# Two stacked transformer blocks on one core: the order of loads and small steps in the first layer's opening

## The chip, the core and the metric

The program runs on one core of a Trainium2 chip. Five engines work side by side, each through its own list of instructions in order: TensorE (PE; its weight loads are shown as PEld), VectorE (DVE), ScalarE (ACT), GpSimd (POOL) and SyncE (SP), which here only issues DMA transfers. ACT and POOL can issue transfers too. The metric is device time in microseconds (us) of one execution.

## What is computed

The reference is a first block of two layers followed by a second block of one layer, all on 256 tokens of width 1024 in float32. Only the opening of the first layer is touched:

```python
# layer 0 of the first block (S = 256 tokens, D = 1024)
h = rmsnorm(x, a_norm_attn);  z = h @ a_w_in           # q, k, v of 6 double heads, and qm
q, k = rope(q), rope(k)
o_self = diff_attention(q, k, v, lam, subln)           # 6 heads
kv = rmsnorm(mem, a_mem_norm) @ a_w_mem_kv             # 256 memory tokens
o_mem = softmax(qm @ mk.T / 8) @ mv                    # 4 memory heads
x = x + concat(o_self, o_mem) @ a_w_out                # then an MLP, layer 1, the second block
```

## The kernel before

**Products.** Every float32 weight tile arrives by DMA as `raw` (128 x 1024 floats, 512 KB, four buffers) and is split into a rounded part `hi` (one ACT instruction, L206) and a remainder `lo` (two DVE instructions, L216). The activations are split in the same way (`hA`, `hMa`, `hMb`: index 0 is the high part, 1 the remainder), and a product is three matmuls: hi by high, hi by remainder, lo by high. One weight tile is one *unit* of 24 matmuls of 256 columns. `tok_block` (L446) yields tokens x features, `feat_block` (L428) features x tokens; each takes two units, and keeps two PSUM tiles until its result is copied out (`evac`).

**Order.** The program has no scheduler at run time: the order in which this Python code emits instructions is the order on each engine. `run_plan` (L228) walks the units. `Order` (L43) holds a clock `O.t` that each matmul advances by its columns / 2.4 ns (four times as much for plain float32, L150), and a queue of generators with due times: `yield 600` means "go on when O.t is 600 ns later", a string means "when this is marked". After each group of matmuls `O.poll()` emits what is due, and at most one piece (hi or half of lo) of a coming weight tile is emitted; the lead over the unit being multiplied grows from 2.25 tiles to 4. `O.need(key)` (L97) emits whatever is queued until the key is marked. A `w_load` follows the last piece of each tile, on SP's queue, where it waits for its buffer.

**The opening before.** `first_inputs` (L895) issues the gains `par` on ACT's queue and, on SP's, x and the first block's weights in turns of two chunks (256 KB each). It emits ten warming matmuls, splits x and these weights two chunks at a time, and spawns:

- `squares`: the squares of x by ACT (L299), summed by POOL (L303, L305) into `ssq_A`; then `tok_stat` and `row_stat` with a delay of 3500, which put tiny products with ones (`mst`, `ms`) on PE and make from them tA (per token, needed to copy v out) and rA (per column, needed for qm, q and k, and by `tables`, four POOL instructions, `ropeR`).
- `second_inputs`: the memory tokens `memT` (1 MB) at once, the rope tables, lambda and constants later.
- `memory_a` at 9200: splits memT to `hMa` chunk by chunk (ACT, then DVE, L277), squares by ACT, sums by POOL (`ssq_M`); then row and token statistics M.
- `lambdas` at 15000; `memory_b` after the memory product.

The units of layer 0 are numbered here from 0: v blocks 0 to 5, qm 6 and 7, memory keys 8 and 9, memory values 10 and 11, then q and k of head h at 12 + 2h, the second layer's memory product, and the output product. A q and k block ends in `rope` (L586): two DVE and two POOL instructions for q, the same for k. `head_a` (the head's scores S, softmax and so on) is due 6500 after its block, `mem_pair` (the memory heads) after heads 0 and 1.

Of the kernel before, what the change touches and what calls it, by code (L numbers as in the profile page):

```python
# [108 lines left out]
def block_kernel(ctx: ExitStack, tc: tile.TileContext, a, out):  # L109
# [60 lines left out]
    def hook(fn):  # L170
        plan.append((len(wlist), 0, fn))

    def w_load(part=(), last=True):
        i = wstate.loaded
        if i >= len(wlist):
            return
        src = wlist[i]
        if i not in wstate.raws:
            wstate.raws[i] = wpool.tile(list(src.shape), F32, tag="raw", name="raw", bufs=RAW)
        sl = (slice(None),) + part  # L180
        nc.sync.dma_start(wstate.raws[i][sl], src[sl])
        wstate.loaded += last

    def w_split(i, part):
# [101 lines left out]


    class Stat:
        def __init__(self, name):
            self.acc = big.tile([P, S], F32, tag="ssq", name="ssq_" + name, bufs=2)  # L290
            self.first = None
            self.n = 0

        def add(self, src, keep=False):
            if keep:
                sq = w_tile("sqk", bufs=KC)
            else:
                sq = wk.tile([P, S], F32, tag="sq", name="sq", bufs=4)
            nc.scalar.activation(sq, src, AF.Square)  # L299
            if self.n == 0:  # L300
                self.first = sq
            elif self.n == 1:
                nc.gpsimd.tensor_tensor(self.acc, self.first, sq, OP.add)  # L303
            else:
                nc.gpsimd.tensor_tensor(self.acc, self.acc, sq, OP.add)  # L305
            self.n += 1
            return sq

# [134 lines left out]
                        O.give("acc", len(c0s))  # L443
            unit([src[:, k0:k0 + per, :]], fn)

    def tok_block(src, cols, h, evac, tile_fn=acc_tile, after=None):  # L446


        def late(dsts, what):
# [6 lines left out]
        for k0 in (0, 4):  # L456
            def fn(w, k0=k0):
                what = "ps" if tile_fn is ps_tile else "acc"
                if k0 == 0:
                    O.take_now(what, 2)  # L460
                    st.ps = [tile_fn("tp") for _ in range(2)]
                x = h()
                for k1 in (k0, k0 + 2):
                    half = w[k1 - k0:k1 - k0 + 2]
                    for j in range(2):
                        dst = st.ps[j][:, 0:cols]
                        ts = slice(j * P, (j + 1) * P)
                        for i, (hi, lo) in enumerate(half):
                            mm(dst, x[:, 0, k1 + i, ts], hi, start=(k1 + i == 0), stop=False)
                            mm(dst, x[:, 1, k1 + i, ts], hi, start=False, stop=False)  # L470
                        yield
                        for i, (hi, lo) in enumerate(half):
                            mm(dst, x[:, 0, k1 + i, ts], lo, start=False, stop=(k1 + i == KC - 1))
                        if j:
                            yield
                if k0 == 4:
                    dsts = [t[:, 0:cols] for t in st.ps]
                    if after:
                        O.spawn(late(dsts, what))
                    else:  # L480
                        for j in range(2):
                            evac(j, dsts[j])
                        O.give(what, 2)
# [410 lines left out]

    def first_inputs():  # L895
        nc.scalar.dma_start(par[:, 0:C_LAM], a["par"][:, 0:C_LAM])
        for i in range(4):
            nc.sync.dma_start(xT[:, 2 * i:2 * i + 2, :], a["xT"][:, 2 * i:2 * i + 2, :])
            w_load((slice(2 * (i % 2), 2 * (i % 2) + 2),), i % 2)
        w_load()  # L900
        w_load()
        E.hA = operand("hA")
        stA = Stat("A")
        warm = ps_tile("warm")
        for _ in range(10):
            nc.tensor.matmul(warm[:, 0:P], ones, ones, start=True, stop=True)
        for k in range(KC):
            split_scaled(E.hA, k, xT[:, k, :], gain(G_A_ATTN, k))
            if k % 2:
                w_split(k // 4, slice(k % 4 - 1, k % 4 + 1))  # L910
        w_piece()
        w_piece()
# [5 lines left out]
        def squares():  # L918
            for k in range(KC):
                stA.add(xT[:, k, :])  # L920
                yield 450
            O.spawn(tok_stat(stA, "A", 3500))
            O.spawn(row_stat(stA, "A", tables, 3500))

        def second_inputs():
            nc.sync.dma_start(memT, a["memT"])
            yield 8100
            nc.sync.dma_start(E.rope_a, a["rope_a"])
            nc.sync.dma_start(par[:, C_LAM:C_END], a["par"][:, C_LAM:C_END])
            nc.sync.dma_start(cst, a["cst"])  # L930

        O.spawn(squares())
        O.spawn(second_inputs())
        E.v = p_tile("vA", (P, 2, 768))
        E.o = operand("oA")
        O.spawn(lambdas(), 15000)
        O.spawn(bias_rows(), 40000)
        O.spawn(memory_a(), 9200)
        O.spawn(memory_b())

    def lambdas():
# [46 lines left out]
    hook(first_inputs)  # L988
    for i in range(3):
        tok_block(a["w_a_v"][i], 256, lambda: E.hA, scaled_tok(lambda: E.v, 256 * i, "tA"),  # L990
                  acc_tile if i else ps_tile, "tA")
    mem_queries(a["w_a_qm"], lambda: E.hA, "rA")
    mem_kv(a["w_a_mem"], wait_for("hMa", lambda: E.hMa), "ma")
    for h in range(6):
        qk_block(a["w_a_qk"][h], lambda: (E.hA, E.hA), wait_for("rA", lambda: E.tr),
                 lambda q, k, h=h: head_a(h, q, k), 6500)
        if h in (0, 1):
            hook(lambda h=h: O.spawn(mem_pair(h, "ma", 6 + h, "oA", PAUSE_MA)))
    mem_kv(a["w_b_mem"], wait_for("hMb", lambda: E.hMb), "mb")

    def staged(first, stat, g, last, name, also=None):
# [574 lines left out]
```

## Time and profile before

| | us |
|---|---|
| timed runs, median of 3 (lowest to highest) | 949.86 (949.54 to 951.19) |
| the profiled execution, its own time | 952.14 |
| its span, first to last instruction | 950.4 |
| TensorE busy in the span | 925.7 |
| first matmul of a product starts | 6.88 |
| output product of layer 0 starts | 128.60 |
| mean granted TensorE clock | 0.991 |

All rows are of the profiled execution; times in them count from its first instruction. An idle time in brackets is that of the engine before the instruction, with what ended it. A matmul of a profile row that names several is a merged run of them (x4), and its time runs from the first start to the last end.

### The profile page before, as it was taken

The numbers are of one execution on the slowest core, as the hardware profiler recorded it, in microseconds if no ns is written. First come the engines' busy times: TensorE is split into PE (matmuls) and PEld (weight loads), VectorE is DVE, ScalarE is ACT, GpSimd is POOL, SyncE is SP. The second block draws the span as 40 slices with busy tenths as digits, with TensorE's granted clock in tenths as the row PEclk, the third lists the DMA queues.
The fourth block names the chain that finished last, engine by engine and source line by source line (L and its number), as shares of the span: only waits on it lengthen the run. The fifth ranks groups of instructions, "written<-read, shape, count | busy, mean of one in ns | idle before, by whom it ended". The sixth has DMA issues, their size and how long they took to land.

```text
span 950.4 us, 17785 instructions
## 1 busy us (share of the span) xinstructions
PE 925.7 (97%) x6800; PEld 856.6 (90%) x6800; DVE 689.2 (73%) x1434; ACT 550.0 (58%) x1063; POOL 198.4 (21%) x236
## 2 busy tenths in 40 slices
PE   7899999999999999999999999999998999999998
PEld 7897898999999998888999999999887989999998
DVE  6978978766666697876866666688956788666664
ACT  6747666655555574656655555566476656555551
POOL 3414633000000032322000000055656411101010
PEclk9899999999999999999999999999999999999999
DMA  8553444665555535332675555574413456655551
GB/s 287 196 178 116 135 152 130 203 203 192 195 188 192 183 131 183 107 109 96 201 241 179 177 181 193 190 257 145 135 62 113 154 154 202 214 193 171 196 201 45
DMA packets 45686, 161.10 MB, mean 170 GB/s; under 512 B 5128, under 2 KB 6800, under 8 KB 45216
## 3 DMA queue, kind: packets, MB, share of 16 engines
q1 hardware_dynamic: 45104, 158.14, 50.6%
q0 software_dynamic: 208, 1.63, 0.6%
q8 instruction: 53, 0.87, 0.4%
q14 instruction: 33, 0.27, 0.1%
q10 hardware_dynamic: 288, 0.18, 0.1%
HBM read 158.88 MB, written 2.63 MB: 170 GB/s over the span
## 4 chain that ended last, share of the span: by engine, by line
PE 82%; DVE 8%; POOL 4%; ACT 2%; issue 2%; DMA 2%; DVEq 0%; SPq 0%; POOLq 0%; ACTq 0%
PE fp L149 41%; PE acc L149 31%; PE tp L149 3%; DVE lo L216 2%; PE S L149 2%; DMA raw<-in_w_a_v_dram 1%; POOL rsh L591 1%; DVE xT L569 1%; ACT hi L206 1%; PE O L149 1%; PE ms L149 1%; PE T L154 1%; PE Sm L149 1%; POOL ssq_A L305 1%; DVE hV L581 1%
## 5 line engine op out<-in xcount | busy, mean ns | idle before, releaser
L216 DVE TENSOR_TENSOR lo<-raw,hi 128x512 fp32r<-128x512 f32 (+1 forms) x555 | 381.8, 734 | 134.2 <-ACT hi L206 133.9
L206 ACT ACTIVATE hi<-raw 128x1024 fp32r<-128x1024 f32 x287 | 296.1, 1053 | 124.1 <-PE fp L149 51.2
L149 PE MATMUL acc<-u,hi 128*128 128x256 f32 x1376 | 245.0, 281 | 0.0
L149 PEld LDWEIGHTS acc<-u,hi 128*128 128x128 f32 x1376 | 210.7, 188 | 0.0
L149 PE MATMUL acc<-u,lo 128*128 128x256 f32 x688 | 193.3, 281 | 0.0
L149 PEld LDWEIGHTS acc<-u,lo 128*128 128x128 f32 x688 | 130.1, 189 | 0.0
L149 PE MATMUL fp<-hW,hi 128*128 128x512 f32 x352 | 96.5, 395 | 1.5 <-DVE uc L424 1.1
L421 ACT ACTIVATE uc<-fp 128x256 f32<-128x256 f32 x108 | 39.9, 380 | 68.9 <-PE fp L149 68.8
L149 PE MATMUL fp<-hV,hi 128*128 128x512 f32 x256 | 70.8, 396 | 0.5 <-DVE hV L581 0.4
L149 PE MATMUL fp<-hU,hi 128*128 128x512 f32 x256 | 70.7, 396 | 0.5 <-DVE hU L581 0.4
L149 PEld LDWEIGHTS fp<-hW,hi 128*128 128x128 f32 x352 | 60.1, 189 | 10.3 <-DVE hW L581 1.6
L424 DVE TENSOR_TENSOR uc<-fp,uc 128x256 f32<-128x256 f32 x108 | 44.2, 420 | 32.8 <-ACT uc L421 31.9
L149 PEld LDWEIGHTS fp<-hW,lo 128*128 128x128 f32 x352 | 53.9, 188 | 7.4
L149 PE MATMUL fp<-hW,lo 128*128 128x256 f32 x352 | 56.1, 282 | 0.0
L149 PEld LDWEIGHTS fp<-hV,hi 128*128 128x128 f32 x256 | 43.8, 189 | 6.9 <-DVE hV L581 1.6
L149 PEld LDWEIGHTS fp<-hU,hi 128*128 128x128 f32 x256 | 43.8, 189 | 6.9 <-DVE hU L581 1.6
L149 PE MATMUL fp<-hZ,hi 128*128 128x256 f32 x304 | 46.8, 294 | 0.4 <-DVE hZ L581 0.4
L857 POOL TENSOR_TENSOR uc<-uc,rstd_W 128x256 f32<-128x256 f32 x22 | 16.1, 754 | 147.8 <-ACT uc L855 147.8
L842 ACT ACTIVATE uu<-uc 128x256 f32<-128x256 f32 x64 | 24.1, 418 | 35.4 <-DVE uc L838 35.4
L149 PEld LDWEIGHTS fp<-hV,lo 128*128 128x128 f32 x256 | 39.2, 188 | 5.5
L149 PEld LDWEIGHTS fp<-hU,lo 128*128 128x128 f32 x256 | 39.2, 188 | 5.4
L564 DVE TENSOR_TENSOR u<-uu,u 128x256 fp32r<-128x256 f32 x64 | 24.4, 422 | 25.5 <-ACT u L562 25.5
(341 smaller groups left out, 1644.5 us busy)
## 6 DMA issues: line engine op xcount, KB each, us to landing
raw<-in_w_a_up_dram SPq DMA_DIRECT2D x32, 512.0 KB, 4.6
raw<-in_w_a_down_dram SPq DMA_DIRECT2D x32, 512.0 KB, 4.4
raw<-in_w_b_up_dram SPq DMA_DIRECT2D x32, 512.0 KB, 4.5
raw<-in_w_b_down_dram SPq DMA_DIRECT2D x32, 512.0 KB, 4.4
raw<-in_w_gate_dram SPq DMA_DIRECT2D x22, 512.0 KB, 4.5
raw<-in_w_up_dram SPq DMA_DIRECT2D x22, 512.0 KB, 4.7
raw<-in_w_down_dram SPq DMA_DIRECT2D x22, 512.0 KB, 4.0
raw<-in_w_a_qk_dram SPq DMA_DIRECT2D x12, 512.0 KB, 3.9
```

Source lines behind the costliest of these rows:

```text
L149: nc.tensor.matmul(dst, lhsT, rhs, **kw)
L154: nc.tensor.transpose(dst, src, ident)
L206: nc.scalar.activation(hi, raw, AF.Copy)
L216: eng.tensor_tensor(lo[sl], raw[sl], f32v(hi[sl]), OP.subtract)
L305: nc.gpsimd.tensor_tensor(self.acc, self.acc, sq, OP.add)
L421: nc.scalar.activation(c, p[:, S:2 * S], AF.Copy)
L424: nc.vector.tensor_tensor(c, p[:, 0:S], c, OP.add)
L564: nc.vector.tensor_tensor(u[:, 1, n, :], us[n], f32v(u[:, 0, n, :]), OP.subtract)
L569: nc.vector.tensor_tensor(x, bank, x, OP.add)
L581: nc.vector.scalar_tensor_tensor(h[:, 1, k, :], xT[:, k, :], g(k), f32v(h[:, 0, k, :]), OP.mult, OP.subtract)
L842: nc.scalar.activation(u, t, AF.Square)
L857: nc.gpsimd.tensor_tensor(g, g, rs, OP.mult)
```

## The change

The opening of the first layer is rearranged; arithmetic and results are the same.

1. The first transfers are smaller and come from two queues: chunk 0 of x and of the weights (128 KB each) on SP, chunk 1 of both on ACT behind `par`; the rest on SP as before.
2. The first v block is split and multiplied chunk by chunk: `w_split` takes chunks 0 and 1 singly, and `fine` makes `tok_block` emit all six matmuls of a chunk before the next.
3. The sums of squares of x go to DVE (`Stat("A", nc.vector)`).
4. `memT` comes in two halves, each 4000 later, behind the tables. `memory_a` is due at 22000 instead of 9200, `lambdas` at 17000 instead of 15000, the statistics A 7600 after the squares instead of 3500.
5. The memory product (keys and values) follows the second q and k block: units 6 and 7 are qm, 8 to 11 the q and k blocks of heads 0 and 1, 12 to 15 memory keys and values. The memory heads start after it and after head 2's block.

```diff
-    def w_load(part=(), last=True):
+    def w_load(part=(), last=True, queue=None):
...
-        nc.sync.dma_start(wstate.raws[i][sl], src[sl])
+        (queue or nc.sync).dma_start(wstate.raws[i][sl], src[sl])
...
-        def __init__(self, name):
+        def __init__(self, name, engine=None):
+            self.engine = engine or nc.gpsimd
...
-                nc.gpsimd.tensor_tensor(self.acc, self.acc, sq, OP.add)
+                self.engine.tensor_tensor(self.acc, self.acc, sq, OP.add)
...
-    def tok_block(src, cols, h, evac, tile_fn=acc_tile, after=None):
+    def tok_block(src, cols, h, evac, tile_fn=acc_tile, after=None, fine=False):
...
-                for k1 in (k0, k0 + 2):
+                for k1 in range(k0, k0 + 4) if fine else ():
+                    hi, lo = w[k1 - k0]
+                    for j in range(2):
+                        dst = st.ps[j][:, 0:cols]
+                        ts = slice(j * P, (j + 1) * P)
+                        mm(dst, x[:, 0, k1, ts], hi, start=(k1 == 0), stop=False)
+                        mm(dst, x[:, 1, k1, ts], hi, start=False, stop=False)
+                        mm(dst, x[:, 0, k1, ts], lo, start=False, stop=(k1 == KC - 1))
+                    yield
+                for k1 in () if fine else (k0, k0 + 2):
...
-        for i in range(4):
+        nc.sync.dma_start(xT[:, 0, :], a["xT"][:, 0, :])
+        w_load((slice(0, 1),), False)
+        nc.scalar.dma_start(xT[:, 1, :], a["xT"][:, 1, :])
+        w_load((slice(1, 2),), False, nc.scalar)
+        for i in range(1, 4):
...
-        stA = Stat("A")
+        stA = Stat("A", nc.vector)
...
-            if k % 2:
+            if k < 2:
+                w_split(0, slice(k, k + 1))
+            elif k % 2:
...
-            O.spawn(tok_stat(stA, "A", 3500))
-            O.spawn(row_stat(stA, "A", tables, 3500))
+            O.spawn(tok_stat(stA, "A", 7600))
+            O.spawn(row_stat(stA, "A", tables, 7600))
...
-            nc.sync.dma_start(memT, a["memT"])
             yield 8100
...
+            for i in range(2):
+                yield 4000
+                nc.sync.dma_start(memT[:, 4 * i:4 * i + 4, :], a["memT"][:, 4 * i:4 * i + 4, :])
...
-        O.spawn(lambdas(), 15000)
+        O.spawn(lambdas(), 17000)
...
-        O.spawn(memory_a(), 9200)
+        O.spawn(memory_a(), 22000)
...
-                  acc_tile if i else ps_tile, "tA")
+                  acc_tile if i else ps_tile, "tA", i == 0)
...
-    mem_kv(a["w_a_mem"], wait_for("hMa", lambda: E.hMa), "ma")
...
-        if h in (0, 1):
-            hook(lambda h=h: O.spawn(mem_pair(h, "ma", 6 + h, "oA", PAUSE_MA)))
+        if h == 1:
+            mem_kv(a["w_a_mem"], wait_for("hMa", lambda: E.hMa), "ma")
+        if h in (1, 2):
+            hook(lambda h=h: O.spawn(mem_pair(h - 1, "ma", 5 + h, "oA", PAUSE_MA)))
```

## Rows read from the trace of the kernel before

**Rows 1.** The page's busy times: us, share of the span, instructions.
```profile
PE 925.7 (97%) x6800; PEld 856.6 (90%) x6800; DVE 689.2 (73%) x1434; ACT 550.0 (58%) x1063; POOL 198.4 (21%) x236
```

**Rows 2.** Stretches: busy of PE, PEld, DVE, ACT, POOL; clock; DMA share; GB/s.
```profile
4.02:7.43 3.41, 1.49 (x12) 1.28 (x11) 1.45 (x3) 2.00 (x5) 0.00 (x0) 1.00 0.90 292
...
7.43:10.85 3.42, 3.42 (x17) 3.24 (x16) 3.00 (x7) 2.98 (x8) 0.00 (x0) 0.50 1.05 373
...
14.41:22.03 7.62, 4.89 (x42) 4.69 (x41) 6.74 (x7) 5.58 (x10) 7.10 (x7) 1.00 0.91 314
...
35.14:41.57 6.43, 4.21 (x34) 3.80 (x32) 6.40 (x13) 4.46 (x8) 5.45 (x8) 1.00 0.37 113
...
41.57:48.40 6.83, 6.42 (x28) 6.24 (x29) 6.66 (x18) 3.25 (x6) 0.00 (x0) 0.50 0.61 191
...
53.46:128.60 75.14, 72.01 (x577) 63.69 (x575) 65.48 (x155) 48.46 (x130) 35.16 (x43) 1.00 0.43 135
...
128.60:950.40 821.80, 808.53 (x5909) 748.96 (x5907) 582.08 (x1202) 467.14 (x868) 144.49 (x168) 1.00 0.51 168
```

**Rows 3.** Waits of TensorE, first 130 us: total us, times, longest.
```profile
PE mst L149 <- POOL ssq_A L305: 2.7, 1, 2.7
...
PE fp L149 <- DVE hMa L277: 2.6, 2, 2.2
```

**Rows 4.** Timeline of TensorE: start, us, instructions (xcount) [idle before].
```profile
14.41 0.64 PE L149 MATMUL tp<-hi,hA 128*128 128x256 f32 x4
...
22.03 0.61 PE L149 MATMUL mst<-ones,ssq_A 128*128 128x2 f32 x4 [2.73 <-POOL ssq_A L305]
...
22.50 0.68 PE L149 MATMUL ms<-ssq_A,ones 128*128 128x256 f32 x2
...
29.65 1.11 PE L149 MATMUL fp<-hA,hi 128*128 128x256 f32 x8
...
35.25 1.11 PE L149 MATMUL fp<-hMa,hi 128*128 128x256 f32 x8
...
43.21 1.05 PE L149 MATMUL ms<-ssq_M,ones 128*128 128x256 f32 x2
...
67.46 0.49 PE L149 MATMUL S<-k,q 64*128 64x128 f32 x4
...
68.84 0.72 PE L149 MATMUL fp<-hA,hi 128*128 128x256 f32 x4
```

**Rows 5.** Timeline of ScalarE, the opening.
```profile
11.19 0.62 ACT L191 ACTIVATE hi<-raw 128x512 fp32r<-128x512 f32 x1
...
24.74 1.57 ACT L800 ACTIVATE vA<-tp,rstdt_A 128x256 f32<-128x256 f32 x4
```

**Rows 6.** Timeline of VectorE, 11 to 36 us.
```profile
11.84 0.69 DVE L192 TENSOR_TENSOR lo<-raw,hi 128x512 fp32r<-128x512 f32 x1
...
23.55 0.68 DVE L216 TENSOR_TENSOR lo<-raw,hi 128x512 fp32r<-128x512 f32 x1
...
24.15 0.16 DVE L329 TENSOR_TENSOR rs4t<-rs4y 128x4 f32<-128x4 f32 x1
...
25.64 0.42 DVE L329 TENSOR_TENSOR rs256t<-rs256y 128x256 f32<-128x256 f32 x1
...
30.34 2.26 DVE L216 TENSOR_TENSOR lo<-raw,hi 128x512 fp32r<-128x512 f32 x2 [0.27 <-ACT hi L206]
...
32.53 0.77 DVE L942 CAST identb<-cst 128x128 bf16<-128x128 f32 x1
...
35.43 0.47 DVE L277 SCALAR_TENSOR_TENSOR hMa<-memT,par,hMa 128x256 fp32r<-128x256 f32 x1
```

**Rows 7.** Timeline of GpSimd, 33 to 63 us.
```profile
33.87 3.78 POOL L305 TENSOR_TENSOR ssq_M<-ssq_M,sq 128x256 f32<-128x256 f32 x4
...
59.32 0.73 POOL L591 TENSOR_TENSOR rsh<-rsh,ropeR 128x256 f32<-128x256 f32 x1 [18.34 <-DVE rsh L590]
...
61.82 1.05 POOL L592 TENSOR_TENSOR k<-rt,rsh 128x256 f32<-128x256 f32 x1
```

More of the change, by code (lines that the diff above doesn't have):

```diff
@@ L302, in add @@
             elif self.n == 1:
-                nc.gpsimd.tensor_tensor(self.acc, self.first, sq, OP.add)
+                self.engine.tensor_tensor(self.acc, self.first, sq, OP.add)
             else:
-                nc.gpsimd.tensor_tensor(self.acc, self.acc, sq, OP.add)
+                self.engine.tensor_tensor(self.acc, self.acc, sq, OP.add)
             self.n += 1
```

## The prediction

> **What bounds the kernel now.** I read the page's busy times first, then a table of stretches, then the waits of TensorE, and last the timelines of the stretches where TensorE waits. TensorE is busy for 925.7 of 950.4 us [rows 1], and of the 821.8 us behind the output product of layer 0 only 13.3 are idle [rows 2]: nothing of the change lies there. What it can win lies ahead of 128.6. Up to 4.02 only warming runs. In 4.02 to 7.43 TensorE is busy 1.49 us and waits 1.92 for the first chunks; the clock then falls to 1.2 GHz (0.50) for 3.41 us, although TensorE is busy throughout [rows 2]. From 14.41 to 22.03 it is busy 4.89 of 7.62 us: it waits 2.7 for GpSimd's sum of squares [rows 2, 3]. From 35.14 to 41.57 it is busy 4.21 of 6.43 and waits for VectorE's remainders of the memory tokens, 2.6 in all, and the clock is at 0.50 for the next 6.83 us [rows 2, 3]. From 53.46 to 128.6 the idle rest is 3.1 us in 75.1 [rows 2]. So the opening loses 2.7 + 2.6 in waits and half of (3.4 + 6.8) to the clock, besides the time until the first product (6.88 in the table). The reader is to see next to it that VectorE was busy for 6.40 of the 6.43 us in which TensorE waited for it [rows 2]: it was not slow with one thing, it was behind with everything.
>
> **1. Opening.** The smaller first transfers and the split by chunks let the first product start earlier, at about 5.5 instead of 6.88. But the first block ends no sooner than its last data. These come in the same bytes at the same rate: the DMA engines are at 0.90 and 1.05 of their time from 4.02 to 10.85 [rows 2], so I count no gain for them. ACT then splits the last two weight chunks from 11.19 to 11.81 and VectorE their remainders to 12.53 [rows 5, 6]. Two of the twelve matmuls of these chunks can run ahead of that; the other ten take 1.2 us (42 matmuls in 4.89, so 0.117 each [rows 2]), which gives 13.7 for the end of the first block, against 14.41 [rows 4]: 0.7 gained. Bounds: nothing, if the chunks are late, or 1.4, if all transfers come 0.7 earlier. ACT's two new issues stand behind `par`, for which its first split waits anyway, and on SP's queue weights move ahead of memT, for which TensorE never waited: both at nothing; if chunk 1 came late, its six matmuls (0.7) would still fit ahead of the last chunks.
>
> The second queue is where the Trainium skill speaks against the change: its page "DMA: Bandwidth & Descriptors", section "Issuing engines are not separate DMA queues", says that transfers issued from several engines run on the same 16 DMA engines, so that a second issuer saves only the time to issue. The full DMA share in the rows agrees; by the page the sum stays as it is.
>
> **2. Squares on VectorE.** Seven additions at 0.42 are 2.9 us more on VectorE, between splits. GpSimd's 7.10 busy us from 14.41 to 22.03 go [rows 2], and with them the slow-down of VectorE beside GpSimd: half a weight tile takes 0.60 from start to start alone (23.55 to 24.15) and 1.13 beside GpSimd (2.26 for two) [rows 6]. Five such splits beside GpSimd give 2.6 back. The edit costs nothing in sum, and the squares are ready by about 19.
>
> The page "SBUF — State Buffer", section "Who interferes with whom", of the Trainium skill states it more strictly: a VectorE instruction with two inputs in SBUF and a GpSimd instruction that reads SBUF exclude each other, and the later one waits for the whole of the other. The rows agree in kind, 0.53 us for each.
>
> **3. Statistics A 4.1 us of planner time later.** By the due times (chunk-wise groups end every 640 ns of O.t, so the eighth square is emitted at 5120, the wait of 7600 begins at 6187 and ends in the group at 13867), `mst` and `ms` come after 10 of the 24 matmuls of unit 5, no longer in unit 3. TensorE gets there at 13.7 + 3 x 2.87 + 1.2 = 23.5, when the sum has long been done: the wait of 2.7 is gone. What is late next is tA. `mst` and `ms` take 0.47 and 0.7 [rows 4]; VectorE's part of `ms` ends at 25.15, and two splits emitted ahead of it (1.2) and three small ones (0.5) bring tA to 26.9. Before, tA was needed long after 24.74 [rows 5], as qm began at 29.65 [rows 4]. Now qm's first PSUM tile is that of the second v block, which ACT copies out third: 26.9 + 2 x 0.36 + 0.47 = 28.1 (four copies in 1.57 [rows 5]). TensorE would be there at 13.7 + 4 x 2.87 + 1.15 = 26.3 and waits 1.8. So qm begins at 28.2, against 29.65: 1.4 gained so far, of 2.7 + 0.7.
>
> **4. Memory later, behind two heads' q and k.** Units 6 to 11 follow without a wait, as weights are split 3 to 4 tiles ahead: two units take 5.6 (29.65 to 35.25 [rows 4]), so unit 11 ends at 45.0. memT's halves are issued behind the tables, at about 25 and 27; the second half landing late is hidden, as ACT needs it after 35.
>
> Now VectorE's list, which decides. From 25.15 to the q and k block of head 1 it must do, by the planner's due times: 16 halves of weight tiles (8 to 15) at 0.60, 9.6; nine instructions on 128 x 256 (three for rA, two for qm, four for `rope` of head 0) at 0.42 [rows 6], 3.8; the two casts and the lambda sums, 2.9 (32.53 to 35.43 [rows 6]); five remainders of hMa at 0.47, 2.35; six small ones at 0.16, 1.0. That is 19.65. Beside it GpSimd has ten instructions that meet these (two of `ropeR`, five sums M, three of `rope`): at 0 to 0.53 each, 0 to 5.3; I take 3.9, near the upper end, since from 35.14 to 41.57 GpSimd was busy 5.45 of 6.43 and VectorE had no idle time [rows 2]. So VectorE comes to `rope` of head 1 at 48.7 (45.0 to 50.1), though its input is there at 45.0.
>
> Behind that stands a queue. Because hMa is not through by unit 12 in planner time (it starts at 22200 and needs 1707 per chunk), `O.need("hMa")` emits chunks 6 and 7 **after** `rope` of head 1. So the last two sums M stand behind four rope instructions on GpSimd. These start 0.85 after VectorE, take 3.55 (59.32 to 62.87), and the two sums 1.9 (four in 3.78) [rows 7]: `ssq_M` is ready at 55.0 (51.3 to 56.4). TensorE meets `ms` of M already after 20 matmuls of unit 12 and the scores of head 0 (1.4: 67.46 to 68.84 [rows 4]): at 45.0 + 2.3 + 1.4 = 48.7. It waits **6.3 us** (2.6 to 7.7) where it now waits 2.6.
>
> Compared at that instruction: before, `ms` of M began at 43.21 [rows 4], with 16 matmuls more of the memory keys done (1.9), without two q and k blocks (11.2) and one head's scores (1.4). The same work would have stood at 43.21 - 1.9 + 11.2 + 1.4 = 53.9. After: 55.0, so 1.1 later (2.6 sooner to 2.5 later). The 1.4 gained are spent.
>
> **5. Clock and rest.** Before, half of 43.21 to 48.40 was lost to the clock, 2.6. After a wait of 6 us I expect the low level again; one stretch at it lasted 3.41 and one 6.83 [rows 2], so 1.7 to 3.4 are lost: no difference counted. The heads' rest moves between units, with the same total work for every engine; the 3.1 us of gaps to 128.6 I leave as they are, by 1.5 either way.
>
> Sum on the profiled execution: 950.4 + 1.1 = 951.5 in span. The timed median, 949.86, is 0.5 below that span, so **951.0**.
>
> **The rivals.**
> - *VectorE is not behind* (faster). If GpSimd's work slots into VectorE's pauses, `rope` of head 1 starts at 45.0, `ssq_M` is there at 51.3 and TensorE waits 2.6. That is 2.6 sooner than before: 947.3. If the clock stays high as well, as it did after the 2.7 us up to 22.03 [rows 2], another 2.6: 944.7. I take 946. For it: the ring lets VectorE run up to four tiles ahead. Against: 6.40 busy of 6.43.
> - *The clock falls in the opening* (slower). Fed in pieces, TensorE idles some 1.7 us between 7.4 and 10.9; before, the clock fell at 7.43 after 1.9 us of idle time [rows 2]. Then the last 20 matmuls of the first block run at half speed, and end at about 15.3 instead of 13.7: all behind moves by 1.6, to 952.6. At 0.08 each, nine matmuls at the low level already take back what the opening gains.
> - *The shared path is dearer* (slower). All ten meetings at 0.53 and the sums behind one more split: `ssq_M` at 56.4 or more, 952.4 upwards; together with the clock 954. The whole GpSimd instruction as the price, as the page on SBUF has it, would add 10 x (0.73 - 0.39) = 3.4, an estimate.
> - *It does not do what it says*: the first block ends at 14.4 as before. 951.7, within the forecast's range.
>
> **How the numbers follow.** 0.2% (1.9 us) is what can be told from no change. Forecast with the fourth rival (0.40): 951.0, its own range 948.5 to 952.5, counted as same. VectorE not behind, 0.24: faster. Low clock in the opening 0.18 and the dearer path 0.18: slower, 0.36. The range from 945.0 to 955.0 leaves out less than 2 in 10.
>
> **What would show it.** Right: no wait for `ssq_A`; about 2 us of TensorE idle before qm, ended by ACT's copy of vA; VectorE reaching the second `rope` 2 to 5 us after its matmuls; 5 to 7 us of idle at `ms` of M, ended by GpSimd. Wrong: TensorE waiting under 3 us there, or waits for hMa in its place; or the output product of layer 0 starting before 126 or after 132.

## The result, and the profile after

| | before | after |
|---|---|---|
| time, us, median | 949.70 | **958.36** |
| the runs | 949.29 to 951.19 | 955.84 to 958.85 |
| ratio | | 1.0082, 95% interval 1.0069 to 1.0095 |
| profiled execution: time; span | 952.14; 950.4 | 958.85; 956.6 |
| second block of layer 0 begins | 14.41 | 17.11 |
| statistics of the memory (`ms` of M) | 43.21, ahead of the heads | 59.36, behind two heads' q and k |
| output product of layer 0 begins | 128.60 | 135.66 |

The change made the kernel slower by 0.82%; 951.0 was forecast, and 958.4 lies outside the range of 945 to 955.

The page's busy times of the kernel after, which answer to [rows 1]: the work is the same, TensorE has 28.6 us without it instead of 24.7.

```profile
PE 928.0 (97%) x6800; PEld 857.7 (90%) x6800; DVE 686.8 (72%) x1442; ACT 549.5 (57%) x1064; POOL 188.6 (20%) x229
```

TensorE's waits in the first 130 us of the kernel after, which answer to [rows 3].

```profile
PE ms L149 <- POOL ssq_M L306: 5.5, 1, 5.5
PE fp L149 <- ACT vA L811: 2.8, 1, 2.8
PE tp L149 <- ACT hi L191: 2.8, 2, 2.2
```

The waits of before (2.7 for `ssq_A`, 2.6 for hMa) are gone, and three others stand in their place, the longest of each over 2 us.

Stretches of the kernel after, with the columns of [rows 2].

```profile
8.50:11.50 3.00, 3.00 (x18) 2.90 (x18) 2.96 (x7) 2.33 (x6) 0.00 (x0) 1.00 0.59 126
...
45.05:53.22 8.17, 8.17 (x76) 7.70 (x74) 8.17 (x15) 5.96 (x13) 7.19 (x8) 1.00 0.54 183
53.22:59.36 6.14, 0.66 (x6) 0.45 (x5) 6.14 (x16) 0.00 (x0) 5.05 (x7) 0.92 0.26 87
59.36:65.23 5.87, 5.87 (x25) 5.69 (x26) 2.44 (x9) 3.69 (x13) 0.59 (x1) 0.50 0.34 98
...
135.66:956.60 820.94, 807.97 (x5907) 748.03 (x5905) 583.27 (x1202) 466.71 (x867) 144.96 (x169) 1.00 0.51 168
```

From the output product on both take nearly the same (820.94 against 821.80). All of the loss of this execution lies ahead of it, 7.1 us. (The spans differ by 6.2, the medians by 8.7; step 6 below comes back to that.) Two places carry it. The first block ends 2.7 later, and in 8.5 to 11.5 the transfers move 126 GB/s. (The clock of 1.00 in that row is not that of the whole stretch: the trace has no clock record ahead of 10.6, and pairs of matmuls take 0.63 us up to 10.5 and 0.40 behind it.) The same stretch of the kernel before:

```profile
8.50:11.50 3.00, 3.00 (x18) 3.00 (x18) 2.62 (x6) 2.67 (x6) 0.00 (x0) 0.61 1.03 373
```

And from 53.22 to 59.36 TensorE has next to nothing to do, while VectorE is busy for all 6.14 us; then the clock is at 1.2 GHz (0.50) for the work that follows.

### The profile page after: what moved, and what is told of

Read it like the earlier page. It is cut to its first block, busy times and chain, and to the rows that moved or that the text cites. A ratio compares the mean times of both kernels' runs of the same rounds, so it can differ in the third digit from the quotient of the medians.

```text
span 956.6 us, 17796 instructions
## 1 busy us (share of the span) xinstructions
PE 928.0 (97%) x6800; PEld 857.7 (90%) x6800; DVE 686.8 (72%) x1442; ACT 549.5 (57%) x1064; POOL 188.6 (20%) x229
## 4 chain that ended last, share of the span: by engine, by line
PE 81%; DVE 9%; DMA 3%; POOL 3%; ACT 3%; issue 1%; SPq 0%; DVEq 0%; POOLq 0%; ACTq 0%
PE fp L149 41%; PE acc L149 31%; DVE lo L216 2%; PE tp L149 2%; PE S L149 2%; ACT hi L206 1%; DVE xT L580 1%; DMA raw<-in_w_a_v_dram 1%; PE ms L149 1%; POOL rsh L602 1%; PE T L154 1%; PE O L149 1%; PE Sm L149 1%; DMA xT<-in_xT_dram 1%; DVE hW L592 1%
## 5 line engine op out<-in xcount | busy, mean ns | idle before, releaser
L216 DVE TENSOR_TENSOR lo<-raw,hi 128x512 fp32r<-128x512 f32 (+1 forms) x555 | 376.7, 725 | 133.3 <-ACT hi L206 132.7
L149 PEld LDWEIGHTS fp<-hZ,hi 128*128 128x128 f32 x304 | 41.0, 195 | 1.8 <-issue 0.7
```

Source lines behind the costliest of these rows:

```text
L149: nc.tensor.matmul(dst, lhsT, rhs, **kw)
L216: eng.tensor_tensor(lo[sl], raw[sl], f32v(hi[sl]), OP.subtract)
```

## The opening: what holds the last weights back

Timeline of SP's queue, kernel after: start, us, engine, line, operation (xcount).

```profile
0.74 0.38 SPq L908 DMA_DIRECT2D xT<-in_xT_dram  x1
1.18 0.42 SPq L181 DMA_DIRECT2D raw<-in_w_a_v_dram  x1
1.65 0.42 SPq L913 DMA_DIRECT2D xT<-in_xT_dram  x1
2.12 0.43 SPq L181 DMA_DIRECT2D raw<-in_w_a_v_dram  x1
2.59 0.43 SPq L913 DMA_DIRECT2D xT<-in_xT_dram  x1
4.20 0.33 SPq L181 DMA_DIRECT2D raw<-in_w_a_v_dram  x1
5.82 0.33 SPq L913 DMA_DIRECT2D xT<-in_xT_dram  x1
6.80 2.99 SPq L181 DMA_DIRECT2D raw<-in_w_a_v_dram  x4
```

And the end of the same list in the kernel before, which had seven issues behind it by then:

```profile
3.07 0.52 SPq L181 DMA_DIRECT2D raw<-in_w_a_v_dram  x1
3.63 0.61 SPq L898 DMA_DIRECT2D xT<-in_xT_dram  x1
4.63 8.26 SPq L181 DMA_DIRECT2D raw<-in_w_a_v_dram  x5
```

The issue that begins the last line of each list is that of the weights of chunks 6 and 7, with which the first block ends: at 4.63 before, at 6.80 after. SP's gaps are waits. Of the issues by line (KB each, median us from issue to landing), two show for what:

```profile
xT<-in_xT_dram SPq DMA_DIRECT2D x1, 128.0 KB, 3.4
raw<-in_w_a_v_dram SPq DMA_DIRECT2D x1, 128.0 KB, 4.6
```

0.74 + 3.4 and 1.18 + 4.6 are 4.1 and 5.8: SP's sixth and seventh issue, at 4.20 and 5.82, follow the landing of its first and second, and its eighth, at 6.80, that of its third (6.78 in the trace). The trace also names what they wait for. All transfers of SP and ACT share eight completion counters that the program deals out, and a transfer waits until the one that had its counter before it has landed. So it is a limit of this program; nothing here shows one of the chip. With the first two pairs cut into four and two pieces on ACT, ACT holds three counters for its own (`par` has the third), and SP gets no further than five. What lands with that is small, so that by 9.5 nothing is under way but what was issued at 6.80 and later, and ScalarE waits:

```profile
14.40 0.63 ACT L191 ACTIVATE hi<-raw 128x512 fp32r<-128x512 f32 x1 [3.57 <-DMA raw<-in_w_a_v_dram]
```

TensorE, at the same place:

```profile
15.08 0.50 PE L149 MATMUL tp<-hi,hA 128*128 128x256 f32 x2 [2.19 <-ACT hi L191]
...
17.11 0.63 PE L149 MATMUL tp<-hi,hA 128*128 128x256 f32 x4
```

Three theories of why the first block ends late: the *full list* (SP can't issue, as all counters are taken); a slow *second queue*; the *order of the product*, chunk by chunk. Four kernels were run to tell them apart.

**The first transfers of before, all else as after.**

```diff
-        nc.sync.dma_start(xT[:, 0, :], a["xT"][:, 0, :])
-        w_load((slice(0, 1),), False)
-        nc.scalar.dma_start(xT[:, 1, :], a["xT"][:, 1, :])
-        w_load((slice(1, 2),), False, nc.scalar)
-        for i in range(1, 4):
+        for i in range(4):
```

> The kernel after, with the four pairs of 256 KB of the kernel before as its first transfers, all from SP; squares, statistics and memory stay as after. Three theories of why the first block of the kernel after ends at 17.1 us and not at 14.4. Full list: SP does not issue while eight transfers are under way, and with the first pairs cut up the last weights of the first block are the eleventh transfer and not the ninth, so they are issued at 6.8 and not at 4.6: here they are issued at 4.6 again, land by 11.5, the first block ends at 13.5 to 14.5, and the time is 958.4 - 2.7 to 3.4 = 955.0 to 955.7. Second queue: what ACT issues is slow or slows the rest: the same numbers here. Order of the product: chunk by chunk and with single-chunk splits it is itself slower: the first block still ends at 16.5 to 17.1, time 958.4.

Measured: 956.38, ratio to before 1.0058 (1.0041 to 1.0075). The second block begins at 14.11. SP's row and ScalarE's of the last weights:

```profile
4.54 8.56 SPq L181 DMA_DIRECT2D raw<-in_w_a_v_dram  x5
```

```profile
11.41 0.62 ACT L191 ACTIVATE hi<-raw 128x512 fp32r<-128x512 f32 x1
```

The product chunk by chunk is not what costs. The 3.0 us gained there came to 2.0 in the time (2.3 by the ratios, which with their intervals leave 0.3 to 4.3), less than the 2.7 to 3.4 expected; where the rest may have gone stands below (the clock).

**Small pieces, all on SP.**

```diff
-        nc.scalar.dma_start(xT[:, 1, :], a["xT"][:, 1, :])
-        w_load((slice(1, 2),), False, nc.scalar)
+        nc.sync.dma_start(xT[:, 1, :], a["xT"][:, 1, :])
+        w_load((slice(1, 2),), False)
```

> The kernel after with its small first transfers, all of them issued by SP in the same order, only the parameters on ACT. Full list: the count is the same, eleven with the parameters, so the last weights of the first block are again issued only when the third has landed, at 6 to 7 us, and land after 13.5: first block ends at 16.5 to 17.5, time 957.5 to 959. Second queue: its price is gone, the last weights land by 11.5, first block ends at 13.5 to 14.5, time 955 to 955.7. Order of the product: 17.1 and 958.4, as full list.

Measured: 957.92 (1.0057 to 1.0101); second block at 16.02. SP is held at its ninth issue and not at its sixth, so the last weights, at the head of the second row, are issued at 5.58, and ScalarE splits them at 12.50:

```profile
5.20 0.33 SPq L913 DMA_DIRECT2D xT<-in_xT_dram  x1
5.58 5.03 SPq L181 DMA_DIRECT2D raw<-in_w_a_v_dram  x4
```

```profile
12.50 0.61 ACT L191 ACTIVATE hi<-raw 128x512 fp32r<-128x512 f32 x1
```

That lies between the theories. How far one execution can be trusted here is told by the other kernels of this document. In the six with the new opening the last weights were issued between 6.51 and 6.80 and landed between 12.71 and 14.37 (the kernel after is the latest); in the eight with the old transfers they were issued between 4.49 and 4.72 and landed between 10.78 and 12.06. With one queue it was 5.58 and 12.32, between both: the second queue and the number of pieces each hold SP back. How much of the time belongs to which isn't shown; 957.92 against 958.36 is within the noise. (The block's end is later than that tells, since the clock was low from 10.88 to 14.29 here.)

**Small pieces from two queues, the last two pairs joined** (nine transfers instead of eleven):

```diff
-        for i in range(1, 4):
-            nc.sync.dma_start(xT[:, 2 * i:2 * i + 2, :], a["xT"][:, 2 * i:2 * i + 2, :])
-            w_load((slice(2 * (i % 2), 2 * (i % 2) + 2),), i % 2)
+        nc.sync.dma_start(xT[:, 2:4, :], a["xT"][:, 2:4, :])
+        w_load((slice(2, 4),))
+        nc.sync.dma_start(xT[:, 4:8, :], a["xT"][:, 4:8, :])
+        w_load()
```

> The kernel after with its four small first transfers from two queues kept, and the last two pairs of 256 KB joined into one of 512 KB for the inputs and one of 512 KB for the weights: nine transfers with the parameters, as before. Full list: only the last one has to wait, for the first landing at 4.2, so the whole half of the weights is issued by 4.5 and lands at 11 to 12; the first block ends at 13.7 to 14.8, time 955 to 956. Second queue: it is still in use, so the last weights land after 13 and the first block ends at 16 to 17, time 957.5 to 958.5. Order of the product: 17, 958.4.

Measured: 957.46 (1.0040 to 1.0086). The profile is of an execution with the granted clock at 0.56 all the way, which says nothing of the block's end; the last weights were issued at 3.81 and landed at 10.42 there. The same kernel once more:

> Again the small first transfers from two queues with the last two pairs joined (nine transfers), since in the profile of the first look the clock was at 0.56 throughout: its last weights landed at 10.4, which speaks for the full list, but the end of its first block can't be compared. Full list: last weights by 11 and first block at 13.7 to 14.8. Second queue: first block at 16 or later.

Measured: 956.29 (1.0043 to 1.0086); second block at 15.10. SP's queue, and ScalarE at the weights of the second half:

```profile
3.69 6.45 SPq L181 DMA_DIRECT2D raw<-in_w_a_v_dram  x4
```

```profile
10.99 0.63 ACT L191 ACTIVATE hi<-raw 128x512 fp32r<-128x512 f32 x1 [0.46 <-DMA raw<-in_w_a_v_dram]
```

With both queues in use but fewer transfers, the last weights are issued at 3.69 and land at 11.0, sooner than in any of the six kernels above, and the second block begins 2.0 sooner than after, 0.3 beyond the range that the full list gave. So the list is what holds the last weights back, and the second queue does so by the counters that it takes from SP, not by what runs on it. The times of this kernel (957.46 and 956.29) are too near to that of after to add to this.

**The new opening alone, on the kernel before.** The edit is the change's own of `first_inputs` and `tok_block`, without the squares on VectorE.

> The kernel before with the new opening alone: small first transfers from two queues, single-chunk splits, first block chunk by chunk. Squares on GpSimd, statistics and memory as before. All three theories put the loss in the opening, so the first block ends at 16.5 to 17.5 here too (the 1 MB of memory tokens is issued early as well and can only add to it). TensorE's wait of 2.7 for GpSimd's sum then shrinks by what the block is later, so the time is between 949.7 (all of it is swallowed by that wait) and 952.4; if the loss of the kernel after is elsewhere, the first block ends at 13.7 and the time is 949 to 949.7.

Measured: 954.65 (1.0032 to 1.0056), second block at 16.83. That is 2.2 above the range expected: the wait for `ssq_A` did shrink, to 1.1, but the wait for the memory operand grew from 2.6 to 3.6. memT is issued behind the late weights (17.54 against 15.31); that this makes the wait grow isn't shown. In the six kernels with this opening the second block begins between 15.4 and 18.0, in the eight with the old transfers between 13.6 and 14.8.

## The other parts, alone and undone

**Squares alone**, on the kernel before (`Stat` takes its engine as in the change):

```diff
-        stA = Stat("A")
+        stA = Stat("A", nc.vector)
```

> The kernel before with the sums of squares of the first layer on VectorE and nothing else changed. Cover theory (step 2 of the prediction): the seven sums cost VectorE 3 us of 0.42 each where it has room, the wait of 2.7 for GpSimd's sum is gone, TensorE reaches the memory product some 2.7 earlier and finds its memory operand no earlier, so the wait of 2.6 there grows to about 5: 949 to 950.3. Price theory: the sums push VectorE's weight splits back, so the waits of the opening grow: over 951.

Measured: 951.35, 1.0018 (1.0006 to 1.0030). TensorE's waits went as the cover theory says, to 4.1 at the memory operand, and no opening wait grew; but the time is that of the price theory, 0.6 to 2.8 longer. The profiled execution doesn't show where (its span is 948.3, under the 950.4 of before). A small part lies outside the span: in every run of this kernel the time is 2.03 to 2.14 above the span, in every run of the kernel before 1.73 to 1.86. What makes these 0.3, and where the rest is, stays open.

**Memory alone**, on the kernel before:

```diff
-            nc.sync.dma_start(memT, a["memT"])
...
+            for i in range(2):
+                yield 4000
+                nc.sync.dma_start(memT[:, 4 * i:4 * i + 4, :], a["memT"][:, 4 * i:4 * i + 4, :])
...
-        O.spawn(lambdas(), 15000)
+        O.spawn(lambdas(), 17000)
...
-        O.spawn(memory_a(), 9200)
+        O.spawn(memory_a(), 22000)
...
+        if h == 1:
+            mem_kv(a["w_a_mem"], wait_for("hMa", lambda: E.hMa), "ma")
```

> The kernel before with the memory alone moved: its tokens fetched in two halves after the tables, its operand started later, its product behind head 1. Step 4 of the prediction: the wait of 2.6 for the memory operand is gone, and a wait of 4 to 6.3 for GpSimd's sum of the memory's squares stands at the matmul of its statistics: +1.1, 950.5 to 951.5. If the memory is what costs the kernel after the rest of its loss (5.5 at that matmul against an equal point of the kernel before), the time is 952 to 955. If the later memory is hidden: 946 to 947.5.

(The memory heads move with it, as in the change.) Measured: 956.74, 1.0069 (1.0048 to 1.0089), above every range given: 6.6 us by the ratio, 7.4 by the medians, and the dearest part. TensorE's waits and two stretches:

```profile
PE ms L149 <- POOL ssq_M L305: 4.7, 1, 4.7
PE mst L149 <- POOL ssq_A L305: 3.2, 1, 3.2
```

```profile
53.00:57.57 4.57, 0.00 (x0) 0.00 (x0) 4.57 (x9) 0.00 (x0) 4.34 (x7) 1.00 0.25 98
57.66:64.49 6.83, 6.83 (x30) 6.58 (x30) 3.35 (x10) 3.69 (x13) 0.51 (x1) 0.50 0.28 84
```

The wait is of the size that step 4 foresaw, but `ms` of M stands at 57.57 and not at 55.0, with the opening of before. The 6.83 us at the low level come behind it. The pieces of this part (transfer in halves, late start of the operand, later product) were not run one by one.

**Memory undone** in the kernel after: the edit above, backwards.

> The kernel after with the memory as in the kernel before: its tokens in one transfer issued early, its operand started early, its product ahead of the heads. Opening, squares and late statistics stay as after. Memory theory: moving the memory alone cost the kernel before 7.4, and that is most of the loss here too; what stays is the opening, which alone cost 4.4, less the wait for GpSimd's sum, gone with the squares on VectorE: 952.5 to 954.7, TensorE's waits at the memory operand being 2.6 to 4. Opening theory: the late last weights are the loss and the memory is even, as step 4 had it: 957 to 958.5.

Measured: 953.83, 1.0028 (1.0013 to 1.0043): 4.5 us back, as the memory theory had it. TensorE doesn't wait for the memory operand at all, since it comes late to it: 3.9 go at qm for vA.

**Both undone**: this and the edit of the first kernel above.

> The kernel after with both the first transfers and the memory of the kernel before; what is left of the change are the squares on VectorE, the late statistics and the first block chunk by chunk. Adding theory: the two undone parts gave 2.0 and 4.6 singly, so 958.4 - 6.6 = 951.8, 951 to 952.5. Overlap theory: what the early end of the opening gives is lost again at the late statistics (ACT's copies of vA are waited for by 3 to 4), as little is gained on undoing the memory alone: 953 to 954.

Measured: 950.89, 1.0012 (1.0001 to 1.0023). The two parts add (951.8 by the sum of what each gave back): with both undone nearly all of the loss is gone. What is left of the change, squares, late statistics and order of the product, costs 0.1 to 2.2 us, though TensorE waits 4.7 for vA here.

**Statistics early**, all else as after:

```diff
-            O.spawn(tok_stat(stA, "A", 7600))
-            O.spawn(row_stat(stA, "A", tables, 7600))
+            O.spawn(tok_stat(stA, "A", 3500))
+            O.spawn(row_stat(stA, "A", tables, 3500))
```

> The kernel after with the first layer's two statistics products 3500 behind the squares as before, not 7600. The sum is there at 22.5, so nothing waits for it, and ACT's copies of vA come some 4 us earlier: the wait of 2.85 at qm falls under 0.5 in any case. If TensorE sets the end at that place, the time falls by 2 to 2.8, to 955.6 to 956.5. If the late memory sets it (its tokens land at 39.5 whatever the statistics do), TensorE is early at the matmul of the memory's statistics and the wait of 5.5 there grows by as much: 957.7 to 958.6.

Measured: 958.76, 1.0095 (1.0076 to 1.0114). The wait for vA is gone, and all of it stands at the next place:

```profile
PE ms L149 <- POOL ssq_M L306: 7.0, 1, 7.0
...
PE fp L149 <- DVE hMa L277: 1.1, 1, 1.1
```

So in the kernel after the wait for vA costs nothing by itself: TensorE comes to `ms` of M at 51.57 instead of 53.88, and that begins at 58.54 instead of 59.36.

## The chain to the memory's statistics

Timeline of GpSimd, kernel after: the two last sums stand behind the four rope instructions of head 1.

```profile
49.54 3.20 POOL L306 TENSOR_TENSOR ssq_M<-ssq_M,sq 128x256 f32<-128x256 f32 x3
54.07 0.72 POOL L602 TENSOR_TENSOR rsh<-rsh,ropeR 128x256 f32<-128x256 f32 x1 [1.32 <-DVE rsh L601]
...
56.59 0.78 POOL L603 TENSOR_TENSOR k<-rt,rsh 128x256 f32<-128x256 f32 x1
57.34 1.97 POOL L306 TENSOR_TENSOR ssq_M<-ssq_M,sq 128x256 f32<-128x256 f32 x2
```

Timeline of VectorE: the rope of head 0 begins at 45.05, that of head 1 at 53.22, and between them a remainder of hMa takes up to 0.96 instead of 0.47 [rows 6], half a weight tile 1.23 instead of 0.68, beside GpSimd.

```profile
45.05 0.41 DVE L600 TENSOR_TENSOR rt<-fp,ropeR 128x256 f32<-128x256 f32 x1
...
46.87 1.23 DVE L216 TENSOR_TENSOR lo<-raw,hi 128x512 fp32r<-128x512 f32 x1
48.02 0.96 DVE L277 SCALAR_TENSOR_TENSOR hMa<-memT,par,hMa 128x256 fp32r<-128x256 f32 x1
...
53.22 0.41 DVE L600 TENSOR_TENSOR rt<-fp,ropeR 128x256 f32<-128x256 f32 x1
```

This piece hardly changes: 8.2 us from rope to rope here, 8.4 with the old transfers, 8.2 with the memory alone, 8.1 with early statistics; and then 6.1 to 6.2 in all four to `ms`, which the complete sum releases. One head's q and k take TensorE 5.6 [rows 4], so it must wait at the end of it. Is that the queue on GpSimd, or VectorE's list?

**Sums of the memory's squares on VectorE**, all else as after:

```diff
-        stM = Stat("M")
+        stM = Stat("M", nc.vector)
```

> The kernel after with the sums of the memory's squares on VectorE too. Queue theory: the last two sums are late because they stand behind four rope instructions on GpSimd (the sum is complete 6.1 behind VectorE's start of the rope of head 1); on VectorE they cost seven times 0.42, 2.9, and free its splits of as many meetings with GpSimd at about 0.5 each, so the sum is ready 1 to 2.5 behind that start, at 53.5 to 55.5: the wait of 5.5 falls to 0 to 1.6 and the time by 4 to 5.5, to 953 to 954.5, and by up to 2.9 more if the clock then stays high. Full-VectorE theory: its list is what is late and gets longer by 2.9: the sum at 57.5 or later, the wait 4 or more, 957 to 958.5.

Measured: 955.77, 1.0053 (1.0040 to 1.0066), 2.6 better than after, and between the two theories. The sum comes 4.5 behind the rope of head 1 instead of 6.1:

```profile
PE ms L149 <- DVE ssq_M L306: 3.9, 1, 3.9
```

Taking the sums out of the queue is worth 1.6 of it. The rest is VectorE, still held up by GpSimd's rope: beside it a remainder of hMa and a sum take up to 0.94 each, where they take 0.47 and 0.41 alone.

**The memory product behind head 2.**

```diff
-        if h == 1:
+        if h == 2:
             mem_kv(a["w_a_mem"], wait_for("hMa", lambda: E.hMa), "ma")
-        if h in (1, 2):
-            hook(lambda h=h: O.spawn(mem_pair(h - 1, "ma", 5 + h, "oA", PAUSE_MA)))
+        if h in (2, 3):
+            hook(lambda h=h: O.spawn(mem_pair(h - 2, "ma", 4 + h, "oA", PAUSE_MA)))
```

> The kernel after with the memory product one head later still, behind head 2. The sum of the memory's squares is ready at 59.3, TensorE comes to its statistics one head (11 us) later than 53.9, so the wait of 5.5 is gone. If that wait is the only thing late there: 953 to 954. If VectorE, 3.4 behind at the rope of head 1, is what is late and the wait was only where it showed, a wait for the rope's q and k (S of head 1 or qk of head 2) takes 2 to 4 of it: 955.5 to 957.5.

Measured: 954.81, 1.0049 (1.0030 to 1.0067), between the two ranges. The wait at `ms` is gone, and one of 2.4 for the k of the rope stands at the scores of a later head than expected, at 98.28:

```profile
PE S L149 <- POOL k L603: 2.4, 1, 2.4
```

**Put together**: the edits of old transfers, early statistics and memory behind head 2.

> Parts put together: the kernel after with the first transfers of the kernel before, the statistics 3500 behind the squares, and the memory product behind head 2; squares stay on VectorE. If the three waits (for the last weights, for vA, for the memory's sum) and the low clock behind them are the loss: from 954.8 (memory behind head 2) less 1.2 in the opening, 3.8 at qm and 1.7 of low clock behind that, 948.1, between 946.5 and 949.5: as fast as the kernel before or a little faster. If VectorE's list is the bound, TensorE only comes earlier to the wait for the rope's k (2.4 at S of head 1 there), which grows to 5 or more: 952 to 954.

Measured: 954.67, 1.0041 (1.0025 to 1.0057). All three waits are gone, and TensorE, early now, waits for the rope:

```profile
PE S L149 <- POOL k L603: 5.7, 3, 2.6
```

That speaks for the second theory, with a time 0.7 above its range. But this is the fastest of the kernel's six executions (951.53), and its output product begins at 128.71, where that of before begins at 128.60: the 3 us up to the median are not in this profile. That VectorE and GpSimd together are the bound of layer 0's heads once the memory's remainders are among them is therefore argued, not shown.

**Less on VectorE's list**, in the kernel before, ahead of its wait for the memory operand:

```diff
-        O.spawn(lambdas(), 15000)
+        O.spawn(lambdas(), 26000)
```

> The kernel before with one number changed: the two casts and the lambda sums of VectorE (2.9 us, from 32.53 to 35.43, in the middle of the memory's remainders) are started 11 us of planner time later, so that they stand behind the last remainder of the memory operand. List theory (in layer 0 VectorE's list sets the end, TensorE only waits where that shows): the wait of 2.6 for the memory operand falls to under 0.5 and the time by 2 to 2.6, to 947 to 947.5, and by up to 3 more where the clock then stays high, 944.5. If what is freed is taken by the same work later, in the heads: 949 to 950, no difference.

Measured: 948.52, 0.9977 (0.9967 to 0.9987), between the two forecasts: an edit of one number makes it faster than the kernel before by 1.2 to 3.1 us. TensorE goes into the memory's product without a wait:

```profile
38.31 1.10 PE L149 MATMUL fp<-hMa,hi 128*128 128x256 f32 x8
...
42.57 0.59 PE L149 MATMUL ms<-ssq_M,ones 128*128 128x256 f32 x2
```

In this execution TensorE came 3.1 later to the product than in [rows 4] (a low stretch at 21.90), so its profile can't say how much of the vanished wait is due to the edit.

**The same with the squares on VectorE.**

> The same on top of the kernel before with its squares on VectorE (951.35, where TensorE waited 4.1 for the memory operand). List theory: 2.9 of that wait go, 947.5 to 948.5; if the clock stays high, 945. Freed time taken later: 950.5 to 951.5.

Measured: 949.30, 0.9994 (0.9984 to 1.0005), 0.24% better against before than the squares alone, 0.8 to 3.8 us with the intervals, where 2.9 us (0.3%) or more were expected. The last remainder of the memory operand on VectorE, with the squares alone and with this edit:

```profile
40.81 0.94 DVE L277 SCALAR_TENSOR_TENSOR hMa<-memT,par,hMa 128x256 fp32r<-128x256 f32 x1
```

```profile
39.16 0.94 DVE L277 SCALAR_TENSOR_TENSOR hMa<-memT,par,hMa 128x256 fp32r<-128x256 f32 x1
```

1.65 of the 2.9 reach the operand. Without the casts between them more of the remainders fall beside GpSimd's sums: they take 0.97, 0.96, 0.94 and 0.94 now, where two of the last four took 0.47. TensorE's wait is only 0.4 shorter (3.8), as it comes 1.0 earlier itself. The list theory holds in direction, with somewhat over half of its price at the operand.

## Why the prediction was wrong, step by step

From 951.0 to 958.4 are 7.4. At `ms` of M 55.0 was forecast and 59.36 came: 4.4. Behind it 896.5 were forecast and 897.2 came: 0.7 (1.6 more up to the output product, 0.9 less from there on). The way from span to median makes the other 2.3. Of the 4.4 the new first transfers have 1.9 (with the old ones `ms` of M stands at 57.42); the other 2.4 belong to steps 3 to 5.

So two steps failed: step 1, which held the new issues to cost nothing, and step 4, which had the mechanism and not the size. All four signs named for a right forecast came: no wait for `ssq_A`, 2.85 idle before qm, VectorE 3.4 behind at the second rope, 5.5 at `ms` of M. Only the last sign of a wrong one came with them, the output product behind 132 (135.66). The signs were of the mechanism, and the loss lay in terms beside it.

**1. Opening: the mechanism was wrong.** "The same bytes at the same rate", and "ACT's two new issues [...] at nothing". 13.7 was forecast, 17.1 came. I priced the transfers by bytes and didn't ask what an issue waits for, though the kernel before has such a wait: SP's eighth issue, at 4.63, stands 0.4 behind the end of its seventh. More pieces push the last one back in a list of fixed length, and the bytes that were to fill the queue aren't asked for. In the time it is 2.0 undone alone, 2.9 undone after the memory (1.5 by the ratios, not clear of the noise), 4.4 alone on the kernel before.

By the sum that went by the Trainium skill ("DMA: Bandwidth & Descriptors", "Issuing engines are not separate DMA queues") the second queue was to bring nothing. The times agree, 957.92 with one queue and 958.36 with two; that it pushes the last issue back, from 5.58 to 6.80, was mine to find.

**2. Squares.** The wait of 2.7 is gone, as said. "Costs nothing in sum" is off by 0.6 to 2.8, and why stays open.

**3. Statistics.** The wait for vA came where it was put, 2.85 against 1.8; the 1.0 more is ScalarE, which waited 2.0 for weights ahead of it. But moving them back (958.76) shows that the wait didn't set the time here.

**4. Memory: mechanism right, term mis-sized.** VectorE came 3.4 behind to the rope of head 1 (3.7 forecast), the two sums did stand behind four rope instructions, TensorE waited 5.5 (6.3 forecast). But +1.1 was the price of the move, and it measured 4.4 to 7.4, by kernel and by whether ratios or medians are taken. Where the opening is as before, `ms` of M stands at 57.4 to 57.6, beyond the upper bound of 56.4. VectorE in the kernel with the old transfers:

```profile
25.15:42.81 17.66, 14.91 (x103) 14.70 (x103) 14.06 (x32) 11.66 (x23) 5.89 (x9) 0.81 0.86 306
42.81:51.26 8.45, 8.45 (x75) 8.32 (x73) 8.16 (x15) 6.61 (x13) 7.15 (x8) 1.00 0.51 171
```

The list was sized well: 14.06 + 8.16 = 22.2 busy from 25.15 to the rope of head 1, against my 23.55. But I let it run without a pause, and it stood idle for 3.9 us, for ScalarE's halves of late weights and for TensorE's q and k. A list that is "behind with everything" from 35 to 41 was not so from 25 on. With these pauses VectorE came to that rope at 51.26, where 48.7 was forecast.

**5. Clock.** One stretch of 6.83 behind the long wait, as in the kernel before: right for this execution. That the second wait, for vA, is one more place for it was left out. With the old transfers:

```profile
28.75:35.57 6.82, 6.15 (x29) 6.15 (x30) 5.12 (x14) 4.43 (x9) 4.22 (x7) 0.50 0.93 365
```

6.15 us of work at half the pace are 3.1 lost. In this execution the 3.0 that the transfers gave back came to 1.9 at `ms` of M; the stretch delays the q and k of head 0, for whose rope VectorE then waits. That this is why the time fell by 2.0 only is argued from one execution.

**6. From span to median.** I took the -0.5 of before (949.86 against a span of 950.4) for the changed kernel as well. The profiled execution of before was itself 2.3 above its median; after stands at 958.36 against 956.6, +1.8, as its profiled execution was only 0.5 above the median. Of the 2.3 between the two offsets 0.5 are not chance: in each run of after the time is 2.20 to 2.25 above the span, and in the one of before 1.74. A median isn't to be tied to one execution's span.

**The rivals.** "VectorE is not behind" (0.24) is out: 8.17 busy of 8.17. "The clock falls in the opening" happened (pairs of matmuls at 0.63 up to 10.5) and cost nothing, as the weights were later still. "The shared path is dearer" is right in kind: remainders at 0.96 for 0.47, splits at 1.23 for 0.68, about 0.5 for each meeting, as in [rows 6]; the page "SBUF — State Buffer" ("Who interferes with whom") of the Trainium skill would have each wait for the whole other instruction, 0.73 where GpSimd's ran alone [rows 7], and the rows show less. No rival held the late weights.

## What to carry to other kernels

Before cutting a transfer into smaller ones, count what may be under way at once and look for the issue that already waits: a piece more at the front is a place less for the piece that ends the stage. Work moved to a later stage is priced by the engine that is shortest there, with its pauses, and by what queues behind it on the next engine; a TensorE wait that vanishes elsewhere says nothing as long as the same chain ends at the next wait. And take the price of each part from the part alone, for here one of three parts was priced at 1.1 and cost 4.4 to 7.4.

## What the runs showed that was not expected

In sixteen profiles there are 25 waits of TensorE of over 2 us ahead of 130 us. With 21 of them came a stretch of 3.41 or 6.83 us at the lower clock, which began inside the wait (11 of them) or at most 1.3 us behind its end (10); one of the four others is the 2.73 of [rows 3] on which the prediction built. What such a stretch costs is half of the work that falls into it, up to 3.4 us, so a wait of 3 us can cost 6.

And a transfer list that has nearly run dry was slow to fill: with 1.25 MB asked for between 6.80 and 7.65, 126 GB/s were moved from 8.5 to 11.5, a third of the 373 of the kernel before. In the six kernels with this opening it was 126 to 238, in the eight with the old transfers 332 to 394, and with the last pairs joined, on both queues, 404. So neither the second queue nor the small pieces make it low by themselves; what does was not separated by a run.

Last, the time isn't the span plus a constant. In the 11 kernels with the sums of x on VectorE and those of the memory on GpSimd it is 2.02 to 2.30 above the span in every execution, in the 5 with both on one engine 1.73 to 1.86. No profile shows what lies outside the span.
